# Low weight parts on VectorE, later copies of weight parts, and one norm per unit, in a hybrid decoder layer

## The chip, the cores and the metric

The kernel runs on one core of a Trainium2 chip, in one launch. The metric is the time on the device of that launch in microseconds (us). The core has five engines with a queue of their own each, worked off in order: TensorE (PE in the profile, with its weight loads as PEld), VectorE (DVE), ScalarE (ACT), GpSimd (POOL), and SyncE (SP), which only issues transfers here.

## The reference

One layer is computed over a sequence of 2048 tokens with 1024 features. Everything is float32.

```python
u = rmsnorm(h, norm_w[l])
proj = (u @ w_in[l]).astype(f32)
(a_q, a_k, a_v, a_gr, a_z, b_q, ..., d_dt, d_z) = jnp.split(proj, split_at, axis=-1)
y_a = gla_branch(...)    # grouped_rmsnorm(o, norm_w, 4) * silu(z)
y_b = mlstm_branch(...)  # grouped_rmsnorm(sigmoid(o_raw) * h, norm_w, 4) * silu(z)
y_c = hgrn2_branch(...)  # grouped_rmsnorm(o, norm_w, 4) * silu(z)
y_d = ssd_branch(...)    # grouped_rmsnorm(y * silu(z), norm_w, 2)
mixed = jnp.concatenate([y_a, y_b, y_c, y_d], axis=-1).astype(h.dtype)
h = h + mixed @ w_out[l]
...
return rmsnorm(h, final_norm_w)
```

Each branch is a causal recurrence over chunks of the sequence. What matters here is that its output is normed by the mean square of each group of 128 columns (256 in the SSD branch) and multiplied by a gate.

## The kernel before

**Tiling.** `run` goes through the sequence in two halves of 1024 tokens (8 chunks of 128). In each half it runs ten units in this order: g0 and g1 (GLA, two heads each), s0 and s1 (SSD), h0 to h3 (HGRN2, a head each), m0 and m1 (mLSTM, two heads each). The output projection (`out_phase`) follows both halves. A unit projects its own columns out of the normed input first, and then does its recurrence.

**Weights.** Each float32 product is made from three products of rounded parts: of the weights `hi` and `lo`, of the input `uh` and `ul`. A unit needs two or three weight tiles of 128 x 8 x 256, 29 in a half. `weights(key)` hands out a tile and starts `load_w` of the next one. In the first half `load_w` loads the tile as it is (`raw`, one buffer), ACT rounds it to `hi` (L242), POOL subtracts to get `lo` (L245; L229 for the first tile, which comes in five pieces), and SP writes both parts to memory (`wk`, L234). In the second half it only loads the two parts back from `wk`. `hi` and `lo` have two buffers each.

**Order.** A framework schedules the instructions when the kernel is built. It takes the order of the code as priority and a model of its own for when an operand is ready, and fixes one order for each engine. The engines then run their queues as they stand and wait on semaphores. While a recurrence waits for ACT or DVE, the scheduler puts projection products of the units that follow into PE's queue.

**Recurrences.** `lin_unit` (GLA and HGRN2) ends in a loop over two groups of four chunks: transposes into `ps_kt`, a copy of them by ACT (L585), products into `ps_u`, four steps of the state by DVE (L593), products into `ps_o`. Then ACT copies `ps_o` out (L606) and `rms` norms it: squares by ACT (L618), a sum over columns by DVE (L620), an inverse root in 13 small DVE instructions (L134 to L139, L621, L622), four products with gate and factor (L611), a transposition (L629) and four transfers to `y`. This is done for each head and group. `mlstm` norms each group with the same `rms`. In `ssd` a chunk is a chain: transposes `ps_xt`, scalings, four decays `t2k` by DVE (L900), an exponential by ACT (L901), a product with `ps_s` (L902), and then PE's `ps_o` and `ps_u`. `finish(g)` norms four chunks, after the fifth chunk and at the end.

PSUM tiles come in two kinds of four banks, `proj` for projections and `t` for the rest. The working tile `t2k` has five buffers, the gate tile `sz` four.

Of the kernel before, what the change touches and what calls it, by code (L numbers as in the profile page):

```python
# [10 lines left out]
F32 = mybir.dt.float32  # L11
# [10 lines left out]
P = 128  # L22
# [6 lines left out]
NC = TH // C  # L29
DI = 2048  # L30
EPS = 1e-6
# [85 lines left out]
class Kernel:  # L117
# [11 lines left out]
    def rsqrt(self, x, w):  # L129

        nc, sm = self.nc, self.small
        y = sm.tile([P, 8], F32, tag="rs_y", name="rs_y")[:, :w]
        t = sm.tile([P, 8], F32, tag="rs_t", name="rs_t")[:, :w]
# [75 lines left out]
    def load_w(self, key, cuts=None):  # L209

        nc = self.nc
# [4 lines left out]
        self.wready[key] = hi, lo  # L216
        if self.ahead_of(key) > 0:
            for t, d in zip((hi, lo), self.wkept[key]):
                nc.sync.dma_start(t.bitcast(F32), d.bitcast(F32))
            return  # L220
# [3 lines left out]
        def part(k0, k1):  # L224
            nc.sync.dma_start(raw[:, k0:k1, :WG], self.a["w"][GIDX[key], :, k0:k1])
            if gates:
                nc.sync.dma_start(raw[:, k0:k1, WG:], self.a["wg"][:, k0:k1])
            nc.scalar.copy(hi[:, k0:k1], raw[:, k0:k1])
            nc.gpsimd.tensor_tensor(lo[:, k0:k1], raw[:, k0:k1], hi[:, k0:k1].bitcast(F32), op=ALU.subtract)  # L229
            keep(k0, k1, 0)  # L230
            keep(k0, k1, 1)

        def keep(k0, k1, i):
            nc.sync.dma_start(self.wkept[key][i][:, k0:k1].bitcast(F32), (hi, lo)[i][:, k0:k1].bitcast(F32))  # L234

        if cuts:
            return [(k0, lambda k0=k0, k1=k1: part(k0, k1)) for k0, k1 in zip(cuts, cuts[1:] + [KT])]
        nc.sync.dma_start(raw[:, :, :WG], self.a["w"][GIDX[key]])
        if gates:
            nc.sync.dma_start(raw[:, :, WG:], self.a["wg"])  # L240
        for k0, k1 in ((0, 2), (2, 4), (4, 6), (6, 8)):
            nc.scalar.copy(hi[:, k0:k1], raw[:, k0:k1])  # L242
        keep(0, 8, 0)
        for k0, k1 in ((0, 4), (4, 8)):
            nc.gpsimd.tensor_tensor(lo[:, k0:k1], raw[:, k0:k1], hi[:, k0:k1].bitcast(F32), op=ALU.subtract)  # L245
        keep(0, 8, 1)

# [185 lines left out]
    def lin_unit(self, nh, f, kb, qp, v, sz, car, eps, ycol, vt=None):  # L433
# [143 lines left out]
        if nh == 1:  # L577
            kr = flip_odd()
        for g in range(2):
            pt = self.psp.tile([P, 4, P], F32, tag="t", name="ps_kt")  # L580
# [23 lines left out]
            for h, po in enumerate(pos):  # L604
                ob = self.t2k().rearrange("p (c d) -> p c d", c=4)
                nc.scalar.copy(ob, po)  # L606
                rs2 = self.rs2[:, 4 * g:4 * g + 4]
                fac = self.rms(ob, eps, rs2)
                nc.vector.tensor_tensor(fac, fac, rs2, op=ALU.mult)
                for c in range(4):  # L610
                    nc.vector.scalar_tensor_tensor(out=ob[:, c], in0=ob[:, c], scalar=fac[:, c:c + 1], in1=sz(h, g)[:, c], op0=ALU.mult, op1=ALU.mult)  # L611
                self.store(ob, g, ycol + h * P)

    def rms(self, ob, eps, fac2):

        nc = self.nc
        sq = self.t2k().rearrange("p (c d) -> p c d", c=4)
        nc.scalar.activation(sq, ob, AF.Square)  # L618
        ss = self.small.tile([P, 8], F32, tag="f_ss", name="f_ss")[:, :4]
        nc.vector.tensor_reduce(out=ss, in_=sq, axis=AX.X, op=ALU.add)  # L620
        nc.vector.tensor_tensor(ss, ss, fac2, op=ALU.mult)  # L621
        nc.vector.tensor_scalar(out=ss, in0=ss, scalar1=1.0 / ob.shape[2], scalar2=eps, op0=ALU.mult, op1=ALU.add)  # L622
        return self.rsqrt(ss, 4)

# [114 lines left out]
    def mlstm(self, h):  # L739
# [17 lines left out]
        N = P + 1  # L757
        fac = self.small.tile([P, 8], F32, tag="m_fac", name="m_fac")
        for g in range(2):
            gs = slice(4 * g, 4 * g + 4)  # L760
# [32 lines left out]
            for u in range(2):  # L793
# [6 lines left out]
                nc.scalar.activation(rd[:, 2 * u:2 * u + 2].unsqueeze(2), po[:, :, P:N], AF.Abs)  # L800
            nc.vector.tensor_tensor(rd, rd, self.thr[:, gs, h], op=ALU.max)
            nc.vector.reciprocal(rd, rd)
            G = to[:, gs]
            nc.vector.scalar_tensor_tensor(out=G, in0=G, scalar=1.0, in1=ob, op0=ALU.add, op1=ALU.mult)
            rd2 = self.small.tile([P, 8], F32, tag="m_rd2", name="m_rd2")[:, :4]
            nc.vector.tensor_tensor(rd2, rd, rd, op=ALU.mult)
            nc.vector.tensor_tensor(rd, rd, self.rs[:, gs], op=ALU.mult)
            nc.vector.tensor_tensor(rd, rd, self.rms(G, 4 * EPS, rd2), op=ALU.mult)
        return to, fac
# [24 lines left out]
    def ssd(self, q):  # L834
# [18 lines left out]
        dD = self.dd[:, h4].unsqueeze(2).to_broadcast([P, 4, 64])  # L853
        def finish(g):
            yb = szs[g]
            ss = self.small.tile([P, 8], F32, tag="s_ss", name="s_ss")[:, :4]
            junk = self.t2k()[:, :256]
            for c in range(4):
                nc.scalar.activation(junk, yb[:, c], AF.Square, accum_out=ss[:, c:c + 1])
            gs = slice(4 * g, 4 * g + 4)  # L860
            nc.vector.tensor_tensor(ss, ss, self.rs2[:, gs], op=ALU.mult)
            nc.vector.tensor_scalar(out=ss, in0=ss, scalar1=1.0 / 256, scalar2=256 * EPS, op0=ALU.mult, op1=ALU.add)
            rs = self.rsqrt(ss, 4)
            nc.vector.tensor_tensor(rs, rs, self.rs[:, gs], op=ALU.mult)
            for c in range(4):
                nc.vector.tensor_scalar(out=yb[:, c], in0=yb[:, c], scalar1=rs[:, c:c + 1], scalar2=None, op0=ALU.mult)
            for j in range(2):
                self.store(yb[:, :, j * P:(j + 1) * P], g, 1536 + 256 * q + j * P)

        for g in range(2):  # L870
            yb = szs[g]
            for u in range(2):
# [3 lines left out]
                for j in range(2):  # L876
# [38 lines left out]
                    nc.vector.tensor_tensor(H, H, pu, op=ALU.add)  # L915
                    if cc == 4:
                        finish(0)
        finish(1)


# [107 lines left out]
    def run(self, units=None, y=None):  # L1028
        nc, tc, a = self.nc, self.tc, self.a
        pool = tc.tile_pool  # L1030
        with pool(name="const", bufs=1) as cp, pool(name="small", bufs=2) as self.small, pool(name="dram", bufs=1, space=DRAM) as self.dram:
# [129 lines left out]
```

## Time and profile before

| | us |
|---|---|
| median of three runs | 2198.5 (2197.16 to 2200.63) |
| the profiled execution | 2200.29 |
| its span, first to last instruction | 2198.2 |
| PE busy | 2108.9 (96%) |
| DVE busy | 1306.8 (59%) |
| ACT busy | 761.0 (35%) |
| POOL busy | 231.1 (11%) |

The profiled execution is the slower end of the three runs within 0.4 us. The first half of the sequence takes the span from 0 to about 953 us, the second half to about 1834 us, and the output projection the rest. In the rows further down, a name such as `lo<-raw,hi` is output and inputs, a line such as L245 is a line of the kernel before, and the tile names are those of the section above.

### The profile page before, as it was taken

The page shows a single profiled execution, that of the slowest core. Times are in us where ns is not written, and L with a number is a line of the kernel's source. Part 1 is how long each engine was busy: PE and PEld are TensorE (multiplying, and loading weights), DVE is VectorE, ACT ScalarE, POOL GpSimd, SP SyncE. Part 2 cuts the span into 40 slices and gives each one's busy share as a digit, 9 for nine tenths or more (in the row PEclk, how much of TensorE's full clock was granted, in tenths as well). Part 3 has the DMA queues.
Part 4 walks back from the last instruction along what each step waited for, and adds up shares of the span by engine and source line. Part 5 has one row for each costly group of instructions (what it writes and reads, how often), then busy time and mean ns, then how long its engine had stood idle before and what let it go on. Part 6 is the DMA issues. An engine that isn't in the chain of part 4 may idle for free.

```text
span 2198.2 us, 35026 instructions
## 1 busy us (share of the span) xinstructions
PE 2108.9 (96%) x13758; PEld 1883.2 (86%) x13758; DVE 1306.8 (59%) x3325; ACT 761.0 (35%) x1643; POOL 231.1 (11%) x223
## 2 busy tenths in 40 slices
PE   7888899999999999999999999999999999999998
PEld 5878788889888898989898898899899998888887
DVE  2475779667766755643748676775564456433332
ACT  4633223334343434435323223433332234322111
POOL 2212123231121112100000101000000000000000
PEclk9999999999999999999999999999999999999999
DMA  8424243342332345362123333321232326432321
GB/s 272 161 85 153 89 138 113 118 144 79 118 117 91 130 135 206 140 185 80 51 87 81 121 78 116 94 81 60 83 112 97 125 73 199 146 106 77 115 72 48
DMA packets 198324, 251.42 MB, mean 114 GB/s; under 512 B 142472, under 2 KB 154360, under 8 KB 179472
## 3 DMA queue, kind: packets, MB, share of 16 engines
q1 hardware_dynamic: 191680, 229.79, 32.5%
q10 hardware_dynamic: 6480, 19.40, 2.5%
q8 instruction: 108, 1.77, 0.3%
q14 instruction: 56, 0.46, 0.1%
HBM read 160.70 MB, written 88.45 MB: 113 GB/s over the span
## 4 chain that ended last, share of the span: by engine, by line
PE 79%; DVE 12%; ACT 4%; DMA 2%; issue 1%; SPq 0%; POOL 0%; ACTq 0%; DVEq 0%; POOLq 0%
PE ps_t L123 27%; PE ps_c L123 20%; PE ps_out L123 16%; PE ps_o L123 6%; PE ps_s L123 5%; PE ps_u L123 2%; PE ps_g L123 2%; DVE t2k L900 1%; DVE kb L512 1%; DMA t2k<-xT 1%; DVE xc L733 1%; DVE qf L513 1%; DVE t2k L611 1%; DMA raw<-w 0%; DVE ST L557 0%
## 5 line engine op out<-in xcount | busy, mean ns | idle before, releaser
L123 PE MATMUL ps_t<-hi,uh 128*128 128x256 f32 x1920 | 545.6, 284 | 0.4 <-DVE craw L729 0.4
L123 PE MATMUL ps_t<-hi,ul 128*128 128x256 f32 x1920 | 544.7, 284 | 0.0
L123 PE MATMUL ps_t<-lo,uh 128*128 128x256 f32 x1920 | 544.6, 284 | 0.0
L123 PEld LDWEIGHTS ps_t<-hi,uh 128*128 128x128 f32 x1920 | 368.8, 192 | 1.7 <-DVE craw L729 0.6
L123 PEld LDWEIGHTS ps_t<-lo,uh 128*128 128x128 f32 x1920 | 368.9, 192 | 0.9
L123 PEld LDWEIGHTS ps_t<-hi,ul 128*128 128x128 f32 x1920 | 368.8, 192 | 0.9 <-issue 0.7
L123 PE MATMUL ps_c<-uh,hi 128*128 128x512 f32 x896 | 357.5, 399 | 11.6 <-ACT uh L155 11.6
L123 PE MATMUL ps_c<-ul,hi 128*128 128x512 f32 x896 | 358.8, 400 | 1.0 <-DVE ul L156 0.9
L123 PE MATMUL ps_c<-uh,lo 128*128 128x512 f32 x896 | 358.5, 400 | 0.0
L123 PEld LDWEIGHTS ps_c<-uh,hi 128*128 128x128 f32 x896 | 170.8, 191 | 45.5 <-ACT uh L155 12.9
L123 PEld LDWEIGHTS ps_c<-ul,hi 128*128 128x128 f32 x896 | 171.3, 191 | 36.9 <-DVE ul L156 2.8
L123 PEld LDWEIGHTS ps_c<-uh,lo 128*128 128x128 f32 x896 | 171.2, 191 | 33.3
L245 POOL TENSOR_TENSOR lo<-raw,hi 128x1024 fp32r<-128x1024 f32 (+1 forms) x58 | 143.2, 2489 | 451.3 <-ACT hi L242 451.2
L972 DVE TENSOR_TENSOR o_sz<-o_sz,ps_out 128x512 f32<-128x512 f32 (+1 forms) x33 | 22.1, 671 | 131.0 <-PE ps_out L123 128.0
L297 ACT ACTIVATE v<-ps_t,ss 128x128 f32<-128x128 f32 x128 | 40.0, 362 | 161.0 <-PE ps_t L123 160.9
L123 PE MATMUL ps_out<-woh,o_qp 128*128 128x512 f32 x288 | 94.3, 396 | 0.0
L293 DVE SCALAR_TENSOR_TENSOR sz<-sz,ps_t 128x256 f32<-128x256 f32 (+1 forms) x80 | 37.7, 471 | 75.3 <-ACT sz L292 74.8
L292 ACT ACTIVATE sz<-ps_t,ss 128x128 f32<-128x128 f32 (+1 forms) x160 | 53.7, 388 | 79.8 <-PE ps_t L123 71.7
L242 ACT CAST hi<-raw 128x512 fp32r<-128x512 f32 (+1 forms) x116 | 65.9, 626 | 37.4 <-PE ps_c L123 20.9
L123 PE MATMUL ps_out<-woh,o_v 128*128 128x512 f32 (+1 forms) x213 | 75.5, 390 | 0.0
L123 PEld LDWEIGHTS ps_out<-woh,o_qp 128*128 128x128 f32 x288 | 54.2, 188 | 12.8
L513 DVE TENSOR_TENSOR qf<-qf,pl 128x512 f32<-128x512 f32 x72 | 54.7, 759 | 17.7 <-PE ps_s L123 9.8
(367 smaller groups left out, 3723.4 us busy)
## 6 DMA issues: line engine op xcount, KB each, us to landing
raw<-w SPq DMA_DIRECT2D x29, 1024.0 KB, 6.9
lo<-wk SPq DMA_DIRECT2D x29, 1024.0 KB, 6.8
hi<-wk SPq DMA_DIRECT2D x29, 1024.0 KB, 6.7
wk<-hi SPq DMA_DIRECT2D x28, 1024.0 KB, 3.9
wk<-lo SPq DMA_DIRECT2D x28, 1024.0 KB, 4.8
y<-t2k SPq DMA_DIRECT2D x256, 64.0 KB, 2.0
t2k<-y SPq DMA_DIRECT2D x64, 256.0 KB, 3.4
t2k<-xT SPq DMA_DIRECT2D x32, 256.0 KB, 4.1
```

The source lines that it names most:

```text
L123: self.nc.tensor.matmul(out, l, r, start=start, stop=stop, skip_group_check=shared)
L242: nc.scalar.copy(hi[:, k0:k1], raw[:, k0:k1])
L245: nc.gpsimd.tensor_tensor(lo[:, k0:k1], raw[:, k0:k1], hi[:, k0:k1].bitcast(F32), op=ALU.subtract)
L292: nc.scalar.activation(out[:, j], ps[:, j], AF.Tanh, scale=self.rsh[:, t + j:t + j + 1])
L293: nc.vector.scalar_tensor_tensor(out=out, in0=out, scalar=1.0, in1=ps, op0=ALU.add, op1=ALU.mult)
L297: self.nc.scalar.activation(out[:, j], ps[:, j], AF.Identity, scale=sc[:, t + j:t + j + 1])
L512: nc.vector.tensor_tensor(kv[:, :, 0], kv[:, :, 0], pv[:, :, 1:2].to_broadcast([P, n, b]), op=ALU.mult)
L513: nc.vector.tensor_tensor(qv[:, :, 1], qv[:, :, 1], pv[:, :, 0:1].to_broadcast([P, n, b]), op=ALU.mult)
L611: nc.vector.scalar_tensor_tensor(out=ob[:, c], in0=ob[:, c], scalar=fac[:, c:c + 1], in1=sz(h, g)[:, c], op0=ALU.mult, op1=ALU.mult)
L733: nc.vector.scalar_tensor_tensor(out=acc, in0=raw[:, k:k + TH], scalar=cw[k], in1=acc, op0=ALU.mult, op1=ALU.add)
L900: nc.vector.scalar_tensor_tensor(out=L[:, h], in0=ab[:, h, j * C:(j + 1) * C], scalar=self.acs[:, cc, 4 * q + h:4 * q + h + 1], in1=self.c ...
L972: nc.vector.tensor_tensor(xt[:, ns], xt[:, ns], ps, op=ALU.add)
```

## The change

`load_w` no longer writes `wk` at once. It leaves a function in `self.unwritten`, which the next `load_w` calls, after it has issued its own load. The subtraction moves from POOL to DVE. In `lin_unit` ACT squares each chunk of `ps_o` in PSUM with a sum over its columns (`squares`), DVE multiplies the gate by `ps_o`, and the inverse root, the factors and the transfers to `y` come once at the unit's end, for all heads and groups. `mlstm` takes its root once per head, `ssd` once per unit, at the end. The tiles of the root are 16 wide.

```diff
@@ load_w
         if self.ahead_of(key) > 0:
+            for k in self.unwritten:
+                k()
+            self.unwritten = []
             for t, d in zip((hi, lo), self.wkept[key]):
...
-            nc.gpsimd.tensor_tensor(lo[:, k0:k1], raw[:, k0:k1], hi[:, k0:k1].bitcast(F32), op=ALU.subtract)
-            keep(k0, k1, 0)
-            keep(k0, k1, 1)
+            nc.vector.tensor_tensor(lo[:, k0:k1], raw[:, k0:k1], hi[:, k0:k1].bitcast(F32), op=ALU.subtract)
...
+        kept, self.unwritten = self.unwritten, [keep]
...
         nc.sync.dma_start(raw[:, :, :WG], self.a["w"][GIDX[key]])
...
+        for k in kept:
+            k()
         for k0, k1 in ((0, 2), (2, 4), (4, 6), (6, 8)):
             nc.scalar.copy(hi[:, k0:k1], raw[:, k0:k1])
-        keep(0, 8, 0)
         for k0, k1 in ((0, 4), (4, 8)):
-            nc.gpsimd.tensor_tensor(lo[:, k0:k1], raw[:, k0:k1], hi[:, k0:k1].bitcast(F32), op=ALU.subtract)
-        keep(0, 8, 1)
+            nc.vector.tensor_tensor(lo[:, k0:k1], raw[:, k0:k1], hi[:, k0:k1].bitcast(F32), op=ALU.subtract)
@@ lin_unit
             for h, po in enumerate(pos):
-                ob = self.t2k().rearrange("p (c d) -> p c d", c=4)
-                nc.scalar.copy(ob, po)
-                rs2 = self.rs2[:, 4 * g:4 * g + 4]
-                fac = self.rms(ob, eps, rs2)
-                nc.vector.tensor_tensor(fac, fac, rs2, op=ALU.mult)
-                for c in range(4):
-                    nc.vector.scalar_tensor_tensor(out=ob[:, c], in0=ob[:, c], scalar=fac[:, c:c + 1], in1=sz(h, g)[:, c], op0=ALU.mult, op1=ALU.mult)
-                self.store(ob, g, ycol + h * P)
+                self.squares(po, ss[:, 8 * h + 4 * g:8 * h + 4 * g + 4])
+                nc.vector.tensor_tensor(sz(h, g), sz(h, g), po, op=ALU.mult)
+        fac = self.rms(ss, P, eps, self.rs2, nh)
...
+        for g in range(2):
+            for h in range(nh):
+                self.scale_rows(sz(h, g), fac[:, 8 * h + 4 * g:8 * h + 4 * g + 4])
+                self.store(sz(h, g), g, ycol + h * P)
+
+    def squares(self, ob, ss):
+
+        junk = self.t2k()[:, :ob.shape[2]]
+        for c in range(4):
+            self.nc.scalar.activation(junk, ob[:, c], AF.Square, accum_out=ss[:, c:c + 1])
+
+    def scale_rows(self, ob, fac):
+        for c in range(4):
+            self.nc.vector.tensor_scalar(out=ob[:, c], in0=ob[:, c], scalar1=fac[:, c:c + 1], scalar2=None, op0=ALU.mult)
@@ ssd
                     nc.vector.tensor_tensor(H, H, pu, op=ALU.add)
-                    if cc == 4:
-                        finish(0)
-        finish(1)
+            self.squares(yb, ss[:, 4 * g:4 * g + 4])
+        finish()
```

At three places the order of the instructions shows what moves. In these rows `ps_c` and `ps_t` are projections, and a number behind x counts equal rows in a run.

The first is SP's queue at the very start, where the first weight tile is loaded in pieces (`raw`) among the input (`xT`). Before:

```order
L225 DMA raw<-w 128x512
L234 DMA wk<-hi 128x256
L153 DMA t2k<-xT 128x512
L234 DMA wk<-hi 128x256
L153 DMA t2k<-xT 128x512
L234 DMA wk<-hi 128x512
L225 DMA raw<-w 128x512
L153 DMA t2k<-xT 128x512 x2
L225 DMA raw<-w 128x512
L234 DMA wk<-hi 128x512
L234 DMA wk<-lo 128x256 x2
```

After:

```order
L228 DMA raw<-w 128x512
L153 DMA t2k<-xT 128x512 x2
L228 DMA raw<-w 128x512
L153 DMA t2k<-xT 128x512 x2
L228 DMA raw<-w 128x512
L153 DMA t2k<-xT 128x512 x5
```

All writes of the first tile's parts now stand behind all loads of `xT` and behind the second tile's load.

The second is DVE's queue in the first half, at the first chunk of s1, where `lo` belongs to the weight tile that comes next. Before:

```order
L892 TENSOR_TENSOR t2k<-ps_xt,g_sp 128x256
L893 TENSOR_TENSOR t2k<-ps_xt,dd 128x256
L293 SCALAR_TENSOR_TENSOR sz<-sz,ps_t 128x512
L900 SCALAR_TENSOR_TENSOR t2k<-ab,g_cs,cf 128x128
L895 TENSOR_TENSOR t2k<-ps_xt,g_de 128x256
L900 SCALAR_TENSOR_TENSOR t2k<-ab,g_cs,cf 128x128 x3
L902 TENSOR_TENSOR t2k<-t2k,ps_s 128x512
```

After:

```order
L901 TENSOR_TENSOR t2k<-ps_xt,g_sp 128x256
L902 TENSOR_TENSOR t2k<-ps_xt,dd 128x256
L297 SCALAR_TENSOR_TENSOR sz<-sz,ps_t 128x512
L250 TENSOR_TENSOR lo<-raw,hi 128x1024
L904 TENSOR_TENSOR t2k<-ps_xt,g_de 128x256
L250 TENSOR_TENSOR lo<-raw,hi 128x1024
L909 SCALAR_TENSOR_TENSOR t2k<-ab,g_cs,cf 128x128 x4
L911 TENSOR_TENSOR t2k<-t2k,ps_s 128x512
```

Both subtractions stand in DVE's queue inside the chunk's chain, and between this chunk's `ps_s` and `ps_o` PE's queue now has 34 projection products where it had 19.

The third is ACT's queue at the end of g0 in the first half, with two heads (two `ps_o` tiles) and two groups. Before:

```order
L585 COPY t2k<-ps_kt 128x512
L606 COPY t2k<-ps_o 128x512
L618 ACTIVATE t2k<-t2k 128x512
L647 COPY qp<-ps_c 128x4x64x2
L242 CAST hi<-raw 128x512
L648 COPY kb<-ps_c 128x512
L242 CAST hi<-raw 128x512 x3
L606 COPY t2k<-ps_o 128x512
L618 ACTIVATE t2k<-t2k 128x512
L297 ACTIVATE o_v<-ps_t,ss 128x256 x2
L585 COPY t2k<-ps_kt 128x512
```

After:

```order
L590 COPY t2k<-ps_kt 128x512
L624 ACTIVATE t2k,f_ss<-ps_o 128x128 x8
L590 COPY t2k<-ps_kt 128x512
L660 COPY qp<-ps_c 128x4x64x2
L248 CAST hi<-raw 128x512 x4
L624 ACTIVATE t2k,f_ss<-ps_o 128x128 x8
```

Eight squares of the first group now stand between the two copies of `ps_kt`, and nothing else does. PE's queue at that place, before, from the second group's transposes on:

```order
L583 MATMUL ps_kt<-cf,kb 128x128 x4
L123 MATMUL ps_c<-uh,lo 128x512
L123 MATMUL ps_c<-uh,hi 128x512
L123 MATMUL ps_c<-ul,hi 128x512
L123 MATMUL ps_c<-uh,lo 128x512
L123 MATMUL ps_c<-uh,hi 128x512
L123 MATMUL ps_c<-ul,hi 128x512
L123 MATMUL ps_c<-uh,lo 128x512
L123 MATMUL ps_c<-uh,hi 128x512
L123 MATMUL ps_c<-ul,hi 128x512
L123 MATMUL ps_c<-uh,lo 128x512
L123 MATMUL ps_t<-hi,uh 128x256
```

After:

```order
L588 MATMUL ps_kt<-cf,kb 128x128 x4
L123 MATMUL ps_c<-uh,lo 128x512
L123 MATMUL ps_c<-uh,hi 128x512
L123 MATMUL ps_c<-ul,hi 128x512
L123 MATMUL ps_c<-uh,lo 128x512
L123 MATMUL ps_c<-uh,hi 128x512
L123 MATMUL ps_c<-ul,hi 128x512
L123 MATMUL ps_c<-uh,lo 128x512
L123 MATMUL ps_c<-uh,hi 128x512
L123 MATMUL ps_c<-ul,hi 128x512
L123 MATMUL ps_u<-o_v,t2k 64x128 x8
L123 MATMUL ps_o<-o_v,ST_93 128x128 x4
```

The `ps_u` products, which read ACT's copy, now follow nine projection products behind the transposes, where 81 stood between them. The later units show the same pattern: in g1 nine where 70 stood, in both halves, and in h0 to h3 of the first half 7 to 14 where 29 to 50 stood.

A fourth shift is told in words: in the second half a load of `lo` stands in SP's queue behind sixteen transfers to `y` that a unit issues together at its end, once behind those of g1 and once behind those of s0, where these came in runs of four and eight.

## Rows read from the trace of the kernel before

**Rows 1.** Busy time by stage: first half, second half, sum (columns: window, its length, engines).

```profile
0.00:960.00 960.00, 894.04 (x6117) 809.58 (x6118) 629.48 (x1505) 381.54 (x826) 192.59 (x151) 0.98 0.41 135
960.00:1834.00 874.00, 858.36 (x6056) 782.14 (x6055) 539.74 (x1451) 296.37 (x661) 38.49 (x72) 0.99 0.31 94
...
sum 2198.20, PE 2108.94 PEld 1883.25 DVE 1306.78 ACT 761.02 POOL 231.08; mean PE 702.98 PEld 627.75 DVE 435.59 ACT 253.67 POOL 77.03
```

**Rows 2.** Timeline of PE: the first matmul (columns: start, length, what, idle before).

```profile
6.03 0.80 PE L123 MATMUL ps_c<-uh,hi 128*128 128x512 f32 x1 [6.03 <-ACT uh L155]
```

**Rows 3.** Chain that ended last: like runs of matmuls in both halves (columns: start, length).

```profile
168.76 37.76 PE ps_t L123 x313
...
934.80 18.71 PE ps_t L123 x156
953.51 10.24 PE ps_c L123 x45
...
1093.69 38.01 PE ps_t L123 x315
...
1815.82 18.71 PE ps_t L123 x156
```

**Rows 4.** PE's waits in the first 70 us (columns: total, times, longest).

```profile
PE ps_c L123 <- ACT uh L155: 10.2, 3, 6.0
```

**Rows 5.** PE's waits from 250 to 550 us, first half.

```profile
PE ps_o L123 <- DVE t2k L902: 14.6, 7, 4.0
```

**Rows 6.** PE's waits from 1190 to 1490 us, the same work in the second half.

```profile
PE ps_o L123 <- DVE t2k L902: 1.3, 4, 0.4
```

**Rows 7.** Timeline of POOL, 308.5 to 317.5 us, first half, a chunk of s1.

```profile
310.16 4.75 POOL L245 TENSOR_TENSOR lo<-raw,hi 128x1024 fp32r<-128x1024 f32 x2 [19.26 <-ACT hi L242]
```

**Rows 8.** Timeline of DVE, the same stretch.

```profile
310.56 4.76 DVE L900 SCALAR_TENSOR_TENSOR t2k<-ab,g_cs,cf 128x128 f32<-128x128 f32 x3
```

**Rows 9.** Timeline of PE, the same stretch.

```profile
316.76 0.99 PE L123 MATMUL ps_o<-t2k 128*128 128x64 f32 x7 [3.76 <-DVE t2k L902]
```

**Rows 10.** DVE's groups by form, first half (columns: busy us, mean ns | idle before).

```profile
L900 DVE SCALAR_TENSOR_TENSOR t2k<-ab,g_cs,cf 128x128 f32<-128x128 f32 x64 | 36.5, 616 | 0.0
...
L156 DVE SCALAR_TENSOR_TENSOR ul<-t2k,par,uh 128x512 fp32r<-128x512 f32 x24 | 17.8, 767 | 19.4 <-ACT uh L155 19.2
```

**Rows 11.** DVE's groups by form, second half.

```profile
L900 DVE SCALAR_TENSOR_TENSOR t2k<-ab,g_cs,cf 128x128 f32<-128x128 f32 x64 | 21.6, 384 | 0.4 <-DMA ab<-rows 0.4
...
L620 DVE TENSOR_REDUCE f_ss<-t2k 128x4 f32<-128x512 f32 x24 | 16.3, 678 | 8.4 <-ACT t2k L618 8.3
...
L138 DVE TENSOR_TENSOR rs_t<-rs_t,rs_y 128x4 f32<-128x4 f32 x84 | 13.5, 161 | 2.1
...
L611 DVE SCALAR_TENSOR_TENSOR t2k<-t2k,rs_y,o_sz 128x128 f32<-128x128 f32 x32 | 9.1, 347 | 0.6
...
L156 DVE SCALAR_TENSOR_TENSOR ul<-t2k,par,uh 128x512 fp32r<-128x512 f32 x8 | 5.6, 747 | 10.2 <-ACT uh L155 10.2
...
L442 DVE TENSOR_TENSOR qf<-qp,f 128x1024 f32<-128x1024 f32 x4 | 5.1, 1263 | 0.1
```

**Rows 12.** POOL's groups by form, whole span.

```profile
L245 POOL TENSOR_TENSOR lo<-raw,hi 128x1024 fp32r<-128x1024 f32 x56 | 137.9, 2483 | 429.8 <-ACT hi L242 429.8
```

**Rows 13.** ACT's groups by form, whole span: squares with a sum, of 256 columns.

```profile
L859 ACT ACTIVATE t2k<-sz 128x256 f32<-128x256 f32 x32 | 13.2, 413 | 4.2 <-POOL sz L913 3.5
```

**Rows 14.** Timeline around the end of an HGRN2 unit in the second half.

```profile
1455.99 0.59 ACT L585 COPY t2k<-ps_kt 128x512 f32<-128x512 f32 x1
...
1459.66 0.58 ACT L606 COPY t2k<-ps_o 128x512 f32<-128x512 f32 x1 [3.09 <-PE ps_o L123]
```

**Rows 15.** SP's queue, 30 to 62 us (columns: start, time to issue).

```profile
41.85 0.33 SPq L234 DMA_DIRECT2D wk<-hi  x1
...
46.40 0.43 SPq L169 DMA_DIRECT2D o_kb<-x  x1
```

**Rows 16.** The page, transfers: KB each, median us to landing.

```profile
lo<-wk SPq DMA_DIRECT2D x29, 1024.0 KB, 6.8
```

More of the change, by code (lines that the diff above doesn't have):

```diff
@@ L131, in rsqrt @@
         nc, sm = self.nc, self.small
-        y = sm.tile([P, 8], F32, tag="rs_y", name="rs_y")[:, :w]
-        t = sm.tile([P, 8], F32, tag="rs_t", name="rs_t")[:, :w]
+        y = sm.tile([P, 16], F32, tag="rs_y", name="rs_y")[:, :w]
+        t = sm.tile([P, 16], F32, tag="rs_t", name="rs_t", bufs=1)[:, :w]
         nc.vector.tensor_scalar(out=t.bitcast(I32), in0=x.bitcast(I32), scalar1=1, scalar2=None, op0=ALU.logical_shift_right)
@@ L228, in part, with keep @@
             nc.scalar.copy(hi[:, k0:k1], raw[:, k0:k1])
-            nc.gpsimd.tensor_tensor(lo[:, k0:k1], raw[:, k0:k1], hi[:, k0:k1].bitcast(F32), op=ALU.subtract)
-            keep(k0, k1, 0)
-            keep(k0, k1, 1)
-        def keep(k0, k1, i):
-            nc.sync.dma_start(self.wkept[key][i][:, k0:k1].bitcast(F32), (hi, lo)[i][:, k0:k1].bitcast(F32))
+            nc.vector.tensor_tensor(lo[:, k0:k1], raw[:, k0:k1], hi[:, k0:k1].bitcast(F32), op=ALU.subtract)
+        def keep():
+            for d, t in zip(self.wkept[key], (hi, lo)):
+                nc.sync.dma_start(d.bitcast(F32), t.bitcast(F32))
+        kept, self.unwritten = self.unwritten, [keep]
         if cuts:
@@ L578, in lin_unit @@
             kr = flip_odd()
+        ss = self.small.tile([P, 16], F32, tag="f_ss", name="f_ss")[:, :8 * nh]
         for g in range(2):
@@ L612, in lin_unit @@
-                self.store(ob, g, ycol + h * P)
-    def rms(self, ob, eps, fac2):
-        nc = self.nc
[L617 to L623, printed above, removed]
+                self.squares(po, ss[:, 8 * h + 4 * g:8 * h + 4 * g + 4])
@@ new lines, in lin_unit @@
+                nc.vector.tensor_tensor(sz(h, g), sz(h, g), po, op=ALU.mult)
+        fac = self.rms(ss, P, eps, self.rs2, nh)
+        f3 = fac.rearrange("p (h c) -> p h c", h=nh)
+        nc.vector.tensor_tensor(f3, f3, self.rs2[:, None].to_broadcast([P, nh, NC]), op=ALU.mult)
+        for g in range(2):
[6 more added lines that the diff above has]
+            self.nc.scalar.activation(junk, ob[:, c], AF.Square, accum_out=ss[:, c:c + 1])
@@ new lines, in scale_rows, with rms @@
+    def scale_rows(self, ob, fac):
+        for c in range(4):
+            self.nc.vector.tensor_scalar(out=ob[:, c], in0=ob[:, c], scalar1=fac[:, c:c + 1], scalar2=None, op0=ALU.mult)
+    def rms(self, ss, n, eps, fac2, nh=1):
+        nc = self.nc
+        s3 = ss.rearrange("p (h c) -> p h c", h=nh)
+        nc.vector.tensor_tensor(s3, s3, fac2[:, None].to_broadcast([P, nh, NC]), op=ALU.mult)
+        nc.vector.tensor_scalar(out=ss, in0=ss, scalar1=1.0 / n, scalar2=eps, op0=ALU.mult, op1=ALU.add)
+        return self.rsqrt(ss, 8 * nh)
@@ L758, in mlstm @@
         fac = self.small.tile([P, 8], F32, tag="m_fac", name="m_fac")
+        ss = self.small.tile([P, 16], F32, tag="f_ss", name="f_ss")[:, :8]
         for g in range(2):
@@ L800, in mlstm @@
                 nc.scalar.activation(rd[:, 2 * u:2 * u + 2].unsqueeze(2), po[:, :, P:N], AF.Abs)
-            nc.vector.tensor_tensor(rd, rd, self.thr[:, gs, h], op=ALU.max)
-            nc.vector.reciprocal(rd, rd)
             G = to[:, gs]
             nc.vector.scalar_tensor_tensor(out=G, in0=G, scalar=1.0, in1=ob, op0=ALU.add, op1=ALU.mult)
[L805 to L808, printed above, removed]
+            self.squares(G, ss[:, gs])
+        nc.vector.tensor_tensor(fac, fac, self.thr[:, :, h], op=ALU.max)
+        nc.vector.reciprocal(fac, fac)
+        rd2 = self.small.tile([P, 8], F32, tag="m_rd2", name="m_rd2")
+        nc.vector.tensor_tensor(rd2, fac, fac, op=ALU.mult)
+        nc.vector.tensor_tensor(fac, fac, self.rs, op=ALU.mult)
+        nc.vector.tensor_tensor(fac, fac, self.rms(ss, P, 4 * EPS, rd2), op=ALU.mult)
         return to, fac
@@ L853, in ssd, with finish @@
         dD = self.dd[:, h4].unsqueeze(2).to_broadcast([P, 4, 64])
[L854 to L868, printed above, removed]
+        ss = self.small.tile([P, 16], F32, tag="f_ss", name="f_ss")[:, :8]
+        def finish():
+            rs = self.rms(ss, 256, 256 * EPS, self.rs2)
+            nc.vector.tensor_tensor(rs, rs, self.rs, op=ALU.mult)
+            for g in range(2):
+                self.scale_rows(szs[g], rs[:, 4 * g:4 * g + 4])
+                for j in range(2):
+                    self.store(szs[g][:, :, j * P:(j + 1) * P], g, 1536 + 256 * q + j * P)
         for g in range(2):
@@ L1052, in run @@
                     self.wkept = {}
+                    self.unwritten = []
                     self.stats = {}
```

## The prediction

> **What bounds the kernel now.** I read the busy times by stage first. PE is busy for 2108.9 of 2198.2 us [rows 1], so what can be won is its idle time and its slower stretches, some 89 us and a little more; everything else matters only where PE waits for it. The two halves compute the same thing, so the second question is where they differ. From the first matmul of the first half to the like matmul of the second it is 953.51 - 6.03 = 947.5 us [rows 2, 3]. Between like runs of matmuls further on the distance shrinks: 1093.69 - 168.76 = 924.9 us, and 1815.82 - 934.80 = 881.0 us [rows 3]. The first half is therefore 66 us slower: 22.6 us are lost up to 168.76, 43.9 us after that. That is the part of the time at which two of the three edits aim.
>
> Then I looked for what makes the first half slow. DVE is busy for 629.5 us there and 539.7 us in the second half [rows 1]. Of these 89.7 us, 12.2 are input conversions that fall into the first half (17.8 against 5.6) [rows 10, 11]; 77.5 us are the same instructions taking longer. L900 shows it: 616 ns against 384 ns in the mean [rows 10, 11]. One place shows why: POOL subtracts two halves of a weight tile from 310.16 to 314.91 us [rows 7], three L900 that begin at 310.56 take 4.76 us [rows 8], and PE stands still for 3.76 us before `ps_o` [rows 9]. Such waits for L902 sum to 14.6 us from 250 to 550 us [rows 5] and to 1.3 us in the like stretch of the second half [rows 6], where POOL subtracts nothing.
>
> **The change part by part.** The sum is made against the profiled execution, 2200.3 us, which is 1.8 us above the median of 2198.5.
>
> *Low parts on DVE.* POOL loses 58 subtractions of 2.48 us [rows 12]; DVE gains them. It did none of this shape into a rounded output, and the nearest row is L442, a product of two SBUF operands of the same 128 x 1024, at 1.263 us [rows 11]: 58 x 1.263 = 73 us. The five small ones at the start stand beside 19.4 us in which DVE waits for ACT's conversions [rows 10] and cost nothing; without that cover they would be some 3 us, by the 0.77 us of a 128 x 512 conversion [rows 10]. So DVE gets 73 us of work and loses 77.5 us of lengthening: by itself nearly nothing in busy time. The subtractions now also stand in DVE's queue, so that what is queued behind them, the decays and products of the SSD chain, waits when ACT's rounding is late. But the order counts with them: the chunk of rows 7 to 9 now has 34 projection products between `ps_s` and `ps_o` for 19, 15 more at 10.24 / 45 = 0.228 us each [rows 3], 3.4 us of work against the stop of 3.76 us [rows 9]. The lengthening was in no order, since an engine's queue is fixed before the run.
>
> *Norms once per unit.* In `lin_unit` a head and group costs DVE a reduction (0.678), 14 small instructions (0.161 each) and four products (0.347 each) [rows 11]: 4.32 us, 16 times in a half, 69 us. Afterwards it is a product of the reduction's size (taken at 0.68) and four scalings (at most 0.347 each), 2.07 us, and 14 small ones once in each of six units: 33 + 14 = 47 us, 22 saved. `mlstm` did a reduction and some 18 small ones eight times (8 x 3.58 = 29 us) and does 18 small ones four times (12 us): 17 saved. `ssd` halves its 14 small ones, 4 times to 2: 4.5 saved. That makes 44 us per half.
>
> *The first half together.* DVE's surplus over the old second half falls from 77.5 to 73 - 44 = 29 us there, to 38%. If PE's loss of 43.9 us goes with it, 27 us are won. The bounds are 0, where the subtractions hold up the same chains as the lengthening did, and 44, where the first half becomes like the second. I take **-27**, as the chunk above points that way: its stop is covered by 3.4 us of new work. What is late next there is the chain itself, which PE met within 0.4 us at most in the second half [rows 6].
>
> *Second half.* DVE gets 44 us lighter, but PE waited there little for it (1.3 us in 300) [rows 6]. I take **-3**, between 0 and -6.
>
> *The gate at the end of GLA and HGRN2 units.* Before, ACT took 0.58 us to copy `ps_o` out [rows 14] and PE had far more filling work before it needed the next group's `ps_kt` copy. Now eight squares of g0's two heads, or one or two of an HGRN2 head, stand before that copy in ACT's queue. A square with a sum takes 0.41 us at 256 columns from SBUF [rows 13]; the trace has none at 128 columns from PSUM. In GLA: 8 x 0.41 + 0.59 for the copy [rows 14] = 3.9 us, less four transposes (some 0.5) and nine projections (9 x 0.228 = 2.05): a stop of 1.3 us; with squares as long as the copy of 512 columns, 0.58 us, 2.7 us. I take 2.2, four units, **+9**. In HGRN2 two squares and the copy less transposes and four projections give 0 to 0.4 us, and DVE's product of gate and `ps_o`, some 0.68 us, stands before the second group's state steps: **1 us in each of eight units, +8**. The bounds are 0, if PE arrives late anyway, and 2.7 x 4 + 2.2 x 8 = 28, where an HGRN2 head also waits for its last two squares (1.2 us). The half of the stops that falls into the first half adds to what the -27 took off.
>
> *Late writes.* In SP's queue the writes of the first tile's parts now stand behind all of `xT`. PE waited 10.2 us for `uh` in the first 70 us, 6.0 of which are the very first wait [rows 4]; that one stays, as nothing is written before it. 4.2 us go, and the `x` loads for the row sums no longer wait behind the second tile's write (they were issued at 46.40, after a write at 41.85 [rows 15]), some 2 us more: **-6**, between -1 and -14, the latter not far from the 22.6 us lost there less the 6.0. Later in the queue the writes still come at much the same places. In the second half two loads of `lo` stand behind sixteen transfers of a unit's end; such a load lands 6.8 us after its issue [rows 16] and was issued with time to spare: **+4**, between 0 and 8.
>
> Sum: -27 - 3 + 9 + 8 - 6 + 4 = -15, so 2200.3 - 15 = 2185, rounded down to **2184 us**.
>
> **What the Trainium skill says against it.** L900, which lengthens, reads two operands from SBUF, and it lengthened while POOL subtracted [rows 7, 8]. The Trainium skill, "SBUF — State Buffer", section "Who interferes with whom", says that VectorE and GpSimd share a pair of ports as an exclusive lock; the rows agree. But the Trainium skill, "Perfetto Trace Analysis", section "Optimizing Scalar/DVE Operations", adds that offloading between those two "might not help". By that rule the first term would be that of the second rival below; 73 us against 77.5 us speak for it, the chunk's new filling against it. The Trainium skill, "PSUM — Partial Sum Buffer", section "PSUM bank collisions raise a hardware error", tells that two engines may not touch a bank at once, even to read; the order has DVE's product wait for ACT's squares on the same `ps_o`, and no row here shows what that costs. It belongs to the third rival.
>
> **The rivals.**
> *All of the lengthening's harm goes* (chance 0.13): the first half becomes like the second and the stops are hidden. 2200.3 - 44 - 3 - 6 = 2147. For it: PE's waits for L902 almost vanish where POOL is quiet [rows 5, 6]. Against it: 73 us of subtractions that the second half never had.
> *A wash* (0.16): DVE's subtractions hold up the chains just as POOL's did, and the norms were off the path. Then the first half wins only 4.5 / 77.5 of 43.9 = 2.5 us; with -6 at the start, half of the stops (8) and no late load: 2200. For it: the two sums of busy time. Against it: the order's filling.
> *Slower by the squares* (0.14): the third term is at its upper bound, since `ps_o` stays taken by four or eight squares and a product in a row and PE's filling before the second group is gone. 28 us of stops, 8 us of late loads, and 10 won in the first half instead of 27, as the first half's units stop as well: 2200.3 + 28 + 8 - 10 - 6 - 3 = 2217. It decides from the point where stops and late loads exceed the 27 + 3 + 6 = 36 us of gains, at 12 stops of 2.7 us with late loads of 4. For it: nine projections where 70 or 81 stood. Against it: ACT is idle for two thirds of the time [rows 1], and most of the stops that I can work out are 1 to 2.4 us.
> *The change does not do what it says*: the writes are late at the start only. Without the start's 6 us the forecast is 2190, inside its own range; it gets no chance of its own.
>
> **How the numbers follow.** The forecast has 0.57; its own range, with the terms moved by about half of their bounds, is 2168 to 2198. A difference under 0.2%, about 4.4 us, cannot be told from none: faster is under 2194, slower above 2203. Of the forecast's 0.57 some 0.05 lie above 2194; of the wash's 0.16, 0.04 below and 0.02 above. Faster: 0.52 + 0.13 + 0.04 = 0.69; slower: 0.14 + 0.02 = 0.16; the same: 0.15. The range takes in half of the first rival and the wash, 2150 to 2205.
>
> **What would show it.** In the profile after: L900's successor at 384 ns in both halves; PE's waits for the SSD product from 250 to 550 us under 4 us instead of 14.6 (right), or about 14 again (the wash); new waits of `ps_u` for the `ps_kt` copy, some 2 us four times and under 1 us eight times (right), or 3 us and more (the third rival); the distance between like runs of the two halves at the start down by 6 and in the rest from 43.9 to about 17. Wrong would be a first half that is still 60 us longer than the second, or a second half longer than before by more than 15 us.

## The result, and the profile after

The changed kernel takes 2163.4 us in the median of four runs (2162.4 to 2164.6), the kernel before 2198.0 beside it: a ratio of 0.9837, 95% interval 0.9825 to 0.9849, or 34.6 us less. The forecast was 2184, 14 us less. The direction was right and the time lies inside the range, but the gain is more than twice the forecast one, and it is made up of other terms.

Busy times by half, with columns as in [rows 1] but cut where the second half begins. First the kernel before (953.5 us, and 1834.5 us for the output projection), then the changed one (894.4 and 1798.4):

```profile
0.00:953.50 953.50, 887.54 (x6088) 804.24 (x6089) 627.40 (x1499) 380.29 (x822) 192.59 (x151) 0.97 0.40 134
953.50:1834.50 881.00, 865.36 (x6089) 787.99 (x6088) 541.81 (x1457) 297.62 (x665) 38.49 (x72) 0.99 0.31 95
```

```profile
0.00:894.40 894.40, 869.99 (x6087) 791.52 (x6088) 572.57 (x1314) 386.34 (x974) 43.25 (x88) 0.99 0.45 143
894.40:1798.40 904.00, 875.29 (x6090) 794.19 (x6089) 501.33 (x1210) 303.65 (x817) 38.45 (x72) 0.98 0.30 93
```

The first half ends 59 us earlier than before (894.4 for 953.5), and the second half takes 23 us longer (904.0 for 881.0); the output projection is within 1 us of the old one. The first column behind the length is PE's busy time, so these rows also split the differences. In the first half PE is idle 41.6 us less (24.4 for 66.0) and busy 17.5 us less with the same matmuls, some of which ran at the lower clock before. In the second half it is idle 13.1 us more (28.7 for 15.6) and busy 9.9 us more. Like runs of matmuls in the chain that ended last, as [rows 3]:

```profile
144.60 46.09 PE ps_t L123 x384
...
874.91 19.68 PE ps_t L123 x164
...
1025.69 46.07 PE ps_t L123 x384
...
1778.73 19.68 PE ps_t L123 x164
```

The distance is 881.1 us early on and 903.8 us at the end: now it is the second half that loses time on the way. DVE's groups in the first half, as [rows 10], and PE's wait from 250 to 550 us, as [rows 5]:

```profile
L250 DVE TENSOR_TENSOR lo<-raw,hi 128x1024 fp32r<-128x1024 f32 x56 | 68.1, 1222 | 15.2 <-ACT hi L248 14.8
...
L909 DVE SCALAR_TENSOR_TENSOR t2k<-ab,g_cs,cf 128x128 f32<-128x128 f32 x64 | 22.4, 394 | 0.6 <-POOL sz L922 0.4 <-DMA ab<-rows 0.2
```

```profile
PE ps_o L123 <- DVE t2k L911: 0.2, 1, 0.2
```

The decays (L909, L900 before) are back at 394 ns, the subtraction costs 1.22 us (1.26 was priced), and the wait for the SSD product fell from 14.6 us to 0.2.

The second half's loss stands at two places. PE's timeline at the first chunk of s0, and its granted clock before, during and after:

```profile
1141.88 0.52 PE L123 MATMUL ps_t<-hi,uh 128*128 128x256 f32 x3
...
1142.83 0.39 PE L123 MATMUL ps_t<-hi,uh 128*128 128x256 f32 x1
1150.59 0.77 PE L123 MATMUL ps_s<-ct,v 128*128 128x128 f32 x2 [7.37 <-DVE ct L749]
...
1154.57 0.78 PE L123 MATMUL ps_t<-lo,uh 128*128 128x256 f32 x1
```

```profile
1100.00:1140.00 40.00, 39.48 (x237) 32.57 (x236) 33.56 (x73) 13.52 (x44) 1.06 (x2) 1.00 0.37 93
1146.00:1159.00 13.00, 7.57 (x32) 7.12 (x33) 5.63 (x11) 1.57 (x2) 0.79 (x1) 0.50 0.18 77
1160.00:1175.00 15.00, 15.00 (x127) 15.00 (x126) 1.74 (x3) 2.52 (x6) 0.74 (x1) 1.00 0.00 1
```

PE stops for 7.4 us, and from 1146 to 1159 us the granted clock is 0.50, that is 1.2 GHz instead of 2.4. The stop reaches into that stretch; PE is busy for 7.57 us of it, of which about half is the price of the lower clock (an estimate by the two clocks: 3.8 us). SP's queue ahead of that place:

```profile
1120.09 0.32 SPq L222 DMA_DIRECT2D hi<-wk  x1
1122.51 9.46 SPq L645 DMA_DIRECT2D y<-t2k  x16
1132.07 0.43 SPq L222 DMA_DIRECT2D lo<-wk  x1
```

The sixteen transfers of g1's end take 9.46 us to issue, and `lo` of the next tile (sz0) comes behind them. It landed 5.1 us after its issue, about 1137, and PE reached the first product with `lo` at 1154.57. So the late load itself stopped nobody. What stopped PE is the order: it puts the SSD chunk's `ps_s` after four projections of sz0, all from `hi` and none from `lo`, and the other 188 behind the chunk's `ps_o`, where all 192 stood before the chunk in the kernel before. That the scheduler did so because it took the load for late is inferred; that the place in SP's queue decides it is tried in run e5. `ps_s` waited for a convolution on DVE (`ct`). The block of norms at g1's end had not held that up, since DVE was idle before it, waiting for its projection:

```profile
1142.08 0.69 DVE L742 TENSOR_TENSOR craw<-ps_c,rb 128x512 f32<-128x512 f32 x1 [1.92 <-PE ps_c L123]
...
1149.21 1.23 DVE L749 SCALAR_TENSOR_TENSOR ct<-th,ct 128x1024 f32<-128x1024 f32 x1 [0.58 <-ACT th L748]
```

From that projection on the convolution takes 8.4 us, and the order gave PE nothing to do beside it. The same happens at s1, where the order has 8 and 1 projections beside the first two chunks instead of 19 and 19, and the 8 again leave `lo` out:

```profile
1268.06 1.96 PE L123 MATMUL ps_o<-t2k 128*128 128x64 f32 x8 [2.03 <-DVE t2k L911]
...
1276.47 1.97 PE L123 MATMUL ps_o<-t2k 128*128 128x64 f32 x8 [3.14 <-DVE t2k L911]
```

```profile
1268.00:1281.00 13.00, 9.80 (x36) 8.36 (x36) 5.71 (x18) 0.89 (x2) 2.12 (x3) 0.50 0.30 83
```

The stops at the two places, 7.4 and 0.8 us at the first and 5.2 at the second, are 13.4 us, about the 13.1 by which PE's idle time grew. The other 9.9 us of the half's 23 are the same matmuls taking longer, as in these two stretches at 1.2 GHz.

### The profile page after: what moved, and what is told of

The parts are those of the page before. It is cut to its first block, busy times and chain, and to the rows that moved or that the text cites. A ratio compares the mean times of both kernels' runs of the same rounds, so it can differ in the third digit from the quotient of the medians.

```text
span 2162.8 us, 34846 instructions
## 1 busy us (share of the span) xinstructions
PE 2101.6 (97%) x13758; PEld 1876.2 (87%) x13758; DVE 1211.3 (56%) x2892; ACT 773.0 (36%) x1947; POOL 81.7 (4%) x160
## 4 chain that ended last, share of the span: by engine, by line
PE 87%; DVE 5%; ACT 4%; DMA 3%; issue 1%; SPq 1%; POOL 0%; ACTq 0%; DVEq 0%
PE ps_t L123 31%; PE ps_c L123 24%; PE ps_out L123 15%; PE ps_o L123 6%; PE ps_s L123 5%; PE ps_u L123 3%; PE ps_g L123 2%; DMA ST<-w_out 1%; DMA t2k<-xT 1%; DVE kb L516 1%; DMA raw<-w 1%; PE ps_xt L898 1%; DVE ST L561 0%; ACT t2k L624 0%; DMA o_f<-x 0%
## 5 line engine op out<-in xcount | busy, mean ns | idle before, releaser
L250 DVE TENSOR_TENSOR lo<-raw,hi 128x1024 fp32r<-128x1024 f32 (+1 forms) x58 | 70.7, 1227 | 16.6 <-ACT hi L248 16.2
L784 DVE TENSOR_TENSOR t2k<-t2k,ps_s 128x512 f32<-128x512 f32 x16 | 11.0, 688 | 103.2 <-PE ps_s L123 99.1
```

The costliest lines, as they stand in the source:

```text
L250: nc.vector.tensor_tensor(lo[:, k0:k1], raw[:, k0:k1], hi[:, k0:k1].bitcast(F32), op=ALU.subtract)
L784: nc.vector.tensor_tensor(dt, dt, ps, op=ALU.mult)
```

## The experiments

Theory A is the prediction's sum. Theory B: what cost time was the lengthening of DVE's instructions beside POOL, because no order counted with it. Theory C, formed on the trace after: the second half loses by the order that follows from `lo` behind sixteen transfers.

**Low parts on DVE alone** (e1), the kernel before with

```diff
-            nc.gpsimd.tensor_tensor(lo[:, k0:k1], raw[:, k0:k1], hi[:, k0:k1].bitcast(F32), op=ALU.subtract)
+            nc.vector.tensor_tensor(lo[:, k0:k1], raw[:, k0:k1], hi[:, k0:k1].bitcast(F32), op=ALU.subtract)
```

> The kernel before with one edit: the low parts come from DVE. Theory A (the prediction's sum: DVE gets 73 us of subtractions for 77.5 us of lengthening, and PE's loss goes with DVE's surplus): the first half wins 2 to 3 us, the whole stays near 2195. Theory B (the lengthening itself was the loss, because no order counted with it, while subtractions on DVE stand in the order and PE gets filling work beside them): the first half wins 35 to 50 us, L900 returns to 380 to 400 ns in the first half, the whole is near 2155. The second half has the old order of instructions and stays at 881 us by both.

2146.7 us, 51.6 less (0.9761, 0.9743 to 0.9779): theory B, a little beyond its bounds (35 to 50 us, near 2155). L900 is back at 380 ns. Busy times by half:

```profile
0.00:901.90 901.90, 874.14 (x6087) 793.18 (x6088) 610.83 (x1561) 380.19 (x822) 43.29 (x88) 0.99 0.43 142
901.90:1782.10 880.20, 864.55 (x6090) 786.96 (x6089) 542.44 (x1459) 298.02 (x665) 38.51 (x72) 1.00 0.31 96
```

DVE is busy for 610.8 us in the first half, hardly less than the 627.4 before, and still 68 us busier than in the second half. Yet the first half takes 902 us from the span's start, where it took 953.5. DVE's busy time was not what PE waited for. PE's order in the first half changed with the edit too, so this run alone doesn't separate the lengthening from the order; run e6 does.

**Late writes alone** (e2), the kernel before with the new `load_w`, the subtraction left on POOL.

> The kernel before with the late writes alone. Both theories: only the first 80 us change. By the prediction's term 6 us less (2192); by the changed kernel's trace, whose gv0 ends 11 us earlier, 9 to 11 us less (2188).

2186.5 us, 11.8 less (0.9946, 0.9931 to 0.9961): twice the prediction's term, and a little more than the changed kernel's trace had said. The run of matmuls that began at 168.76 us [rows 3] begins 10.7 us earlier:

```profile
158.06 38.91 PE ps_t L123 x313
```

In the profile the second half, whose order of matmuls is the same, is 3.6 us shorter too (877.4 for 881.0); that is no effect of the edit that the trace shows.

**Norms once per unit alone** (e3), the changed kernel with the old `load_w`.

> The kernel before with norms once per unit alone. Theory A: 44 us less DVE work in the first half wins some 25 us there; the second half loses what it loses in the changed kernel, 23 us; the whole is near 2196. Theory B: the norms were off the path, the first half wins 0 to 10 us and the second half loses 23 us; the whole is 2210 to 2221.

2208.1 us, 9.8 more (1.0042, 1.0027 to 1.0057). The halves show both sides:

```profile
0.00:940.10 940.10, 884.69 (x6088) 802.62 (x6088) 582.41 (x1251) 387.78 (x974) 193.27 (x151) 0.97 0.40 136
940.10:1842.70 902.60, 873.24 (x6090) 792.28 (x6089) 501.38 (x1211) 304.09 (x818) 38.45 (x72) 0.98 0.31 93
```

The first half wins 13 us, the second loses 22. In the first half that lies between the two theories (25, and 0 to 10): while POOL lengthens DVE's instructions, a lighter DVE is worth something.

**All but the norms** (e4): late writes and low parts on DVE, the norms as before.

> The changed kernel without the norms once per unit (late writes and low parts on DVE stay). Theory A: the first half loses the norms' 25 us, the second half regains 23: near 2165. Theory B: the second half goes back to 881 us and the first half keeps nearly all of its 59 us: 2140 to 2150, faster than both kernels.

2136.0 us, 62.2 less than before (0.9715, 0.9701 to 0.973) and 27.4 less than the changed kernel, below even theory B's 2140 to 2150. The edits of e1 and e2 add up (51.6 + 11.8 = 63.4). The norms cost 26 us in the second half (904.0 for 878.0) and 4 in the first (894.4 for 890.6): once POOL is quiet, DVE's lighter load (40 us in each half by the traces, 44 in the prediction) is worth nothing.

**`lo` through another queue** (e5), the changed kernel with

```diff
-            for t, d in zip((hi, lo), self.wkept[key]):
-                nc.sync.dma_start(t.bitcast(F32), d.bitcast(F32))
+            for t, d, e in zip((hi, lo), self.wkept[key], (nc.sync, nc.gpsimd)):
+                e.dma_start(t.bitcast(F32), d.bitcast(F32))
```

> The changed kernel with one edit: in the second half the low parts are loaded through POOL's queue instead of SP's, so that no transfer to y stands before them. Theory C (the second half loses its 23 us because the loads of lo stand behind sixteen transfers in SP's queue, and the order therefore keeps projections away from PE at two places): the order has its 192 and 19 projections back at both places, both stops and the slow stretches behind them go, the whole falls by 20 to 26 us, to 2138 to 2144. Theory D (the norms themselves lose it: squares on PSUM, a long block of DVE work at a unit's end): the second half stays near 904 us and the whole near 2163.

2138.1 us (0.9728, 0.9714 to 0.9743), 25.4 less than the changed kernel: theory C. The norms are the same, and so is the block of DVE work at a unit's end; the order has its 192 projections ahead of s0's first chunk and 19 beside each of the first two chunks of s1 again, and the list of PE's waits from 1100 to 1160 us is empty. So the place of these loads in SP's queue decides the order.

**The norm of SSD's first chunks early** (e9), in the changed kernel (the calls are shown; `finish` is that of the kernel before):

```diff
-            self.squares(yb, ss[:, 4 * g:4 * g + 4])
-        finish()
+                    if cc == 4:
+                        finish(0)
+        finish(1)
```

> The changed kernel with the SSD norm of the first four chunks back after the fifth chunk; GLA, HGRN2 and mLSTM keep the new norms. By theory C each of the two places in the second half has its own burst of transfers: the place in sz1 to hqf0 belongs to SSD's sixteen and goes (two waits of 5.2 us in sum and 13.7 us at the lower clock, some 12 us), the place in sz0 belongs to GLA's sixteen and stays (some 14 us): 2150 to 2154. If both hang on one cause, both go (2138) or stay (2163).

2158.4 us (0.9805, 0.9786 to 0.9825; one of four runs took 2151.1), 5 less than the changed kernel, not the 9 to 13 of the forecast. The second place is gone (1.2 us of waits from 1240 to 1300 us for 5.8, and no slow stretch), the first stands with its 7.4 us. In the profile the second half wins 9.5 us, and the first, where the early norms stand as well, loses 2.3. So each place does have its own transfers, but the gain of the whole was overstated.

**POOL at work for nothing** (e6), run e4 with a second subtraction whose result nobody uses, behind DVE's:

```diff
             nc.vector.tensor_tensor(lo[:, k0:k1], raw[:, k0:k1], hi[:, k0:k1].bitcast(F32), op=ALU.subtract)
+            nc.gpsimd.tensor_tensor(raw[:, k0:k1], raw[:, k0:k1], hi[:, k0:k1].bitcast(F32), op=ALU.subtract)
```

> The kernel without the new norms (run e4) in which POOL subtracts as well, from raw into raw, after DVE has made lo from it: POOL's result is used by nothing, the order of PE's instructions is the same to the row. Theory B (the lock between POOL's and DVE's operands is the loss): L900 and its like lengthen again in the first half by 40 to 75 us in sum, PE waits for the SSD product as before, and the whole rises by 20 to 45 us, to 2156 to 2181. Rival (the loss was that POOL's parts came late, at 2.4 us each behind the rounding, and only the order was bad): DVE lengthens, but PE does not wait, and the whole stays at 2136 to 2142.

2199.0 us (1.000, 0.9991 to 1.001), 63 more than run e4: the whole gain of late writes and DVE's parts is gone, although PE's order is e4's to the row (DVE's and ACT's differ in the place of one instruction each). The first half in run e4, then in run e6:

```profile
0.00:890.60 890.60, 865.24 (x6088) 788.29 (x6089) 612.28 (x1561) 381.40 (x822) 43.11 (x88) 0.99 0.46 144
```

```profile
0.00:952.70 952.70, 887.06 (x6087) 805.63 (x6088) 694.92 (x1561) 380.67 (x822) 202.62 (x146) 0.97 0.42 134
```

DVE's busy time rises by 83 us. Of PE's 62 us, 40 are idle time (65.6 for 25.4) and 22 are the same matmuls taking longer at the lower clock. DVE's subtractions and the `kb` products there, in run e4, then in run e6, and last PE's longest waits in run e6 from 250 to 550 us:

```profile
L250 DVE TENSOR_TENSOR lo<-raw,hi 128x1024 fp32r<-128x1024 f32 x56 | 68.1, 1225 | 3.8 <-ACT hi L248 3.5
L516 DVE TENSOR_TENSOR kb<-kb,pl 128x512 f32<-128x512 f32 x36 | 24.9, 693 | 3.2 <-PE ps_s L123 3.2
```

```profile
L250 DVE TENSOR_TENSOR lo<-raw,hi 128x1024 fp32r<-128x1024 f32 x55 | 87.5, 1598 | 3.3 <-ACT hi L248 2.9
L517 DVE TENSOR_TENSOR kb<-kb,pl 128x512 f32<-128x512 f32 x36 | 29.6, 821 | 3.2 <-PE ps_s L123 3.2
```

```profile
PE ps_o L123 <- DVE t2k L907: 9.2, 4, 3.9
PE ps_o L123 <- DVE craw L730: 3.6, 1, 3.6
```

Run e4 has 0.4 us of the first wait there. POOL's work stops PE, through DVE. That POOL also holds `raw` longer explains little: DVE's subtractions waited 3.3 us in all for ACT's rounding (3.8 in run e4), and PE 1.2 us for `lo`. Two things were not as expected. The size was again underrated, at 20 to 45 us. And the decays hardly lengthen here (410 ns for 376), because POOL now works behind DVE's subtraction and runs beside other instructions.

**Writes of the first tile behind the loads of x** (e7), run e4 with these writes called after the loop of `row_stats`.

> Run e4 with the writes of the first tile's parts moved behind the loads of x for the row sums. If the wait of ps_rb (6.5 us, and a slow stretch of 10.2 us behind it, in run e4) is due to x standing behind these writes, it shrinks by 4 to 6 us and the whole falls by 5 to 11 us, to 2125 to 2131; if ACT's rounding of the next tile is what ps_rb waits for, nothing changes (2136).

2134.6 us (0.9708, 0.9693 to 0.9722), 1.4 less than run e4, and well under the 5 to 11 of the first reading. Its mechanism holds, though: the wait of `ps_rb` shrinks from 6.5 to 2.1 us, and the first half ends at 886.6 for 890.6. The second half gives 3.8 of it back, with the same stops, at a lower clock (last section).

**Both queues' edits with the new norms** (e8: changed kernel, e5 and e7).

> The changed kernel with both edits of runs e5 and e7. If theory C holds and the edits add up: 2128 to 2138, near run e7, so that norms once per unit are worth nothing by themselves, as PE does not wait for DVE; if DVE's 44 us less per half count, it is 5 us or more below run e7.

2134.7 us (0.9707, 0.9692 to 0.9721), the same as e7 with the old norms. But e7 loads `lo` through SP's queue; the comparison that differs by the norms alone is with the next run.

**The same without the new norms** (e10: e7 with `lo` through POOL's queue).

> Late writes, low parts on DVE, the old norms, the writes of the first tile behind the loads of x, and the second half's low parts through POOL's queue. If the old norms leave nothing for the other queue to mend, as run e4's second half of 878 us says, it is run e7 again, 2132 to 2137; a difference of over 3 us either way would show a cost or a gain of POOL's queue itself.

2130.9 us (0.9689, 0.9673 to 0.9706), 3.7 less than e7. One thing POOL's queue does mend: PE's wait for `lo` in gv0 of the second half (1.8 us in e7) is gone. The second half in run e7, then in run e10:

```profile
886.60:1768.40 881.80, 867.05 (x6090) 789.94 (x6089) 542.11 (x1460) 297.55 (x665) 38.49 (x72) 0.99 0.31 95
```

```profile
889.20:1764.80 875.60, 861.96 (x6089) 785.39 (x6088) 542.03 (x1459) 297.94 (x665) 54.28 (x101) 1.00 0.31 96
```

PE's idle time there falls by only 1.1 us, its busy time by 5.1 at a higher clock, and the first half is 2.6 us longer in the same order. So a gain of POOL's queue itself is not shown beyond that one wait. Run e8 is 3.8 us slower than this one: the new norms are worth nothing by themselves. This is the fastest kernel here, 1.5% below the changed one.

## Why the prediction was wrong

It reached the right sign through a sum of mis-sized terms; two large errors partly cancelled.

1. *The first half together* (-27) is the step that failed. It let PE's loss go with DVE's surplus of busy time, so that 38% of the loss stayed. Run e1 shows 51.6 us won while DVE's busy time in the first half falls by only 17, and run e6 brings the loss back in the same order of matmuls. The bound of 44 from the first rival was the better reading: what PE waited for was time that the order did not know of. That bound left out the time before 168.76 us, where e1 wins 5.5 us as well (the first `ps_kt` at 139.5 us for 145.0). The sign that I gave for the term was misread. The chunk of [rows 7] to [rows 9] is the first of s0, not of s1, and in the changed kernel it has 21 projections for 19, 0.5 us of filling against its stop of 3.76 us. The 34 for 19 belong to the first chunk of s1, whose stop was 4.0 us. Both stops are gone (0.2 us is left of the second), so the first went without filling, because the decays no longer lengthen. The 77.5 us of lengthening came from windows of unlike length; cut where the halves meet, it is 627.4 - 541.8 - 12.2 = 73.4, which changes the term little. Stops also cost more than their length where a stretch at 1.2 GHz follows: 17.5 of the 59 us won in the first half are busy time.
2. *Norms in the first half*: inside that term 44 us of DVE work counted as a gain. They win 13 us while POOL subtracts (e3) and lose 4 when it doesn't (changed kernel against e4).
3. *The gate at the unit's end* (+17) did not come. In the trace after, ACT at the end of g1 in the second half, and PE:

```profile
1107.76 0.28 ACT L624 ACTIVATE t2k<-ps_o 128x128 f32<-128x128 f32 x1 [4.43 <-PE ps_o L123]
...
1108.02 0.27 ACT L624 ACTIVATE t2k<-ps_o 128x128 f32<-128x128 f32 x1
...
1109.77 0.64 ACT L590 COPY t2k<-ps_kt 128x512 f32<-128x512 f32 x1
```

```profile
1110.45 1.09 PE L123 MATMUL ps_u<-o_v,t2k 128*64 128x128 f32 x16 [0.17 <-ACT t2k L590]
```

   Eight squares take 2.0 us, 0.25 each, not the 0.41 to 0.58 of the rows I took; nine projections cover them and the copy, and the stop is 0.17 us. All waits for that copy sum to 1.2 us in the whole run. The Trainium skill, "PSUM — Partial Sum Buffer", section "PSUM bank collisions raise a hardware error", has two engines kept off one bank; the order does keep DVE's product behind the squares, and that cost PE nothing that the trace shows.
4. *Late loads* (+4, 0 to 8) is the other step that failed: the place was right, the size was 23 to 26 us, and the mechanism was another. I priced the transfer, which came in time. What cost was the order built around it, which moved filling work away, and the slow clock behind the stops (e5). A second half more than 15 us longer was the prediction's own sign of being wrong.
5. *Late writes* (-6): 11.8 by e2. Mechanism right, half the size, inside its bounds.
6. *Second half lighter* (-3): nothing; in PE's idle time of the second half e8 and e10, which differ by the norms alone, agree to 0.2 us.
7. Measured terms: -51.6 for DVE's parts, -11.8 for the writes and +27.4 for the norms, with the late loads that they cause, are -36.0, against -34.6.

The rule against the change, the Trainium skill, "Perfetto Trace Analysis", section "Optimizing Scalar/DVE Operations", that offloading between GpSimd and VectorE might not help, fits the sums of busy time (e1) but not the time: 51.6 us were won. The exclusive lock, in the Trainium skill, "SBUF — State Buffer", section "Who interferes with whom", agrees with e6, where POOL's useless subtraction lengthens DVE's to 1.6 us and costs 63.

What stays open: which of the lengthened DVE instructions cost PE most, since neither the trace nor a run separates them, and by what rule the scheduler moves projections when a load stands late in SP's queue.

## What to carry to other kernels

An engine's busy total says little where the order is fixed beforehand: price what the order did not count with, and look for it as an instruction that takes longer in one stage than in another. When work is gathered at a unit's end, look at what its burst of transfers stands in front of, and at what order the scheduler then builds; moving that load to another queue was worth 25 us here. Norms on an engine that nobody waited for were worth nothing here, at 40 us less DVE work in each half.

## What the hardware showed unexpectedly

A square of 128 columns from PSUM with its sum is issued every 0.25 us on ACT, less than the 0.41 us that one of 256 columns, twice as wide and from SBUF, showed [rows 13].

Not every DVE instruction lengthens beside POOL's subtraction. Counted in the trace of the kernel before, the 12 decays (L900, two tiles in SBUF) that ran beside one took 1650 ns in the mean, the other 116 took 381. Of L791, the same operation of mLSTM on `st` with `ps_u` in PSUM, 12 ran beside one as well, and they took 349 ns like the rest.

Equal stops were followed by different clocks. Run e7, then run e4, in each the stretch behind the same stop of 2.2 us before `ps_s` in the second half:

```profile
988.50:991.90 3.40, 3.18 (x15) 3.21 (x16) 1.64 (x5) 0.81 (x2) 0.61 (x2) 0.50 0.00 0
```

```profile
991.60:995.00 3.40, 3.36 (x23) 3.13 (x24) 2.56 (x6) 1.87 (x4) 0.61 (x2) 1.00 0.02 5
```

PE had done the same work in the same order and stopped for 2.20 and 2.19 us; in one trace 3.4 us at 1.2 GHz follow, in the other none. Over the whole second half run e7 is busy 4.1 us longer than run e4 with the same matmuls (867.05 for 862.97) and idle no longer. A gain of 4 us at the start was lost that way, so differences of a few microseconds between such kernels should not be given a cause.
